# Dummy products at the start, an earlier end of attention, and block sums held back, in a hybrid flow step on one core

## The chip, the cores and the metric

The kernel runs on one core of a Trainium2 chip. The metric is the device time of one launch in microseconds (us). A core has five engines that this text names by the profile's words: PE (matrix products), DVE and ACT (vector and scalar work), POOL (a slower vector engine, which here also issues some DMAs) and SP (which issues most DMAs).

## The reference, cut to what matters

The program is one inference step of two layers over 640 tokens (512 latent tokens in a grid of 8 x 64, and 128 prompt tokens) of width 1024. All data are float32. Layer 0 mixes tokens by attention, layer 1 by a gated linear recurrence; a gated feed-forward stage (width 2816) follows each.

```python
def layer(ctx, lat, i):
    # six modulation vectors per group: silu(cond) @ w_mod[i] + b_mod[i]
    xm_c, xm_l = modulate(rms_norm(ctx)), modulate(rms_norm(lat))   # shift and scale
    if i == 0:
        # prompt: softmax(q k^T / 8) v over the 128 prompt tokens, 16 heads of 64
        # latent: softmax over a window of 8 rows x 16 columns (+ bias table)
        #         and over 256 cached keys of the context
        o_c, o_l = attention(xm_c, xm_l, cache_k, cache_v) # then @ attn_w_o
    else:
        o_c, o_l = recurrent_block(xm_c, xm_l, state_h)    # then @ lru_w_out
    ctx, lat = ctx + g1 * o_c, lat + g1 * o_l
    for x in (ctx, lat):                                   # feed-forward
        gate, up = split(modulate(rms_norm(x)) @ w_gu[i])
        x += g2 * ((silu(gate) * up) @ w_down[i])
```

The outputs are both groups of tokens after a last norm, the new keys and values of the prompt, and the last states of the recurrence.

## The kernel before

Activations lie transposed: eight tiles of 128 features by 640 tokens (`x`), and a product is made in two chunks of 320 tokens. A float32 product is made as three products of a shorter type: each operand is split into a high part (a cast, on ACT) and a low part (operand less high part, on DVE), and PE adds high x high, high x low and low x high (`some`, L221 to L223; `split`, L1305). One such instruction of 320 columns follows the last after 0.147 us.

**The start** (`pe` at L318, `act` at L324, `dve` at L321 record each instruction in the order in which it is written). While `x` arrives, PE adds up squares for the norm. The first four vectors of modulation come from `vectors` (16 products of 256 columns for each of two halves `h` and two kinds `j`, one of each as soon as its weights `sw` have landed), are copied by ACT to `row` and brought into columns by `coefficients` (products `at<-sel,row`). The squares are summed over features by five products of `ssq` with a column of ones (`at<-ones,ssq`), DVE and POOL make the reciprocal root `rs` and the diagonal tiles `dg`, and `spread` brings them to all partitions (`kk<-dg,ones`). `normed` on DVE and `high` on ACT then make the first operand of the first real products. `keep(2)` issues two products of the conditioning vector with the identity, into columns of `aux` that nobody reads.

**Attention** goes over eight pairs of heads `p`. For each, `qk` makes queries and keys of the pair, and splits them: casts `KS<-K` on ACT (L796), low parts into `KZ` on DVE (L797), and a DMA that brings each half to the other partitions (L799; on POOL's queue for pairs 0 and 7). `attend` goes over four blocks of 128 latent tokens, two at a time: for each block scores (L821, L822), score read on DVE (L827), exponential on ACT (L830), scaling, four transposes (L839) and their copy `PT` on ACT (L841). `softmax_prompt` does the like for the prompt's 128 tokens (L856 to L869), and `heads_out` multiplies with the values (`op`, L917) and copies to `O`. The first output products with `wo` stand behind the last pairs: `O` of the first seven pairs is split into `ohi` and `olo` after pair 6, pinned behind `self.parted`, the last key cast and the last low part of pair 7, so that the splits of the output do not come ahead of what pair 7 waits for. `project` then multiplies with `wo`; three output tiles are accumulated at once while pair 7 is still in its softmax.

**The feed-forward stage of layer 1** is made by halves with block sums: `x` is cut into four blocks (features 0 to 511 and 512 to 1023, tokens 0 to 319 and 320 to 639: B11, B12, B21, B22). `second_half(k)` splits B12 and B22 of tile `k` (`halve`), and `sums(k)` makes differences of the blocks on DVE (L999 to L1001) and POOL (L1002, `t4`), which are split too. `sum_weights` makes sums of the weights' blocks on POOL (L1057), behind `t4` of the second tile (`self.pw`). The products are at L1136 to L1138.

What stands in which order on an engine is set by the order of the source, by a scheduler that moves ready work of one engine ahead by its own estimate of time, and by pins (`pin`, `issue_after`): an instruction so marked comes behind the one named. Each engine then works its queue in that order, and an instruction that waits holds all behind it.

Of the kernel before, what the change touches and what calls it, by code (L numbers as in the profile page):

```python
# [125 lines left out]
class _Step:  # L126
# [169 lines left out]
    def start(self, hi, lo, sp, big):  # L296
# [97 lines left out]
        dve(nc.vector.tensor_scalar, v, aux[:, 256:256 + NT], 1.0 / D, EPS, ALU.mult, ALU.add)  # L394
# [5 lines left out]
        vectors(0, pm, 1, 1)  # L400
        row = rows(0, pm)
# [40 lines left out]
        keep(2)  # L442
# [147 lines left out]

    def project(self, w, hi, lo, gk, nxt=None, done=None, ahead=False):
        G = self.need(self.gcols, gk)
        for f in range(KT):
            u = self.unit(w[f], "m" if ahead else None)
            for t0, t1 in CH:
                self.residual(f, t0, t1, self.chunk(u, hi, lo, t0, t1, not ahead or f > 1), G, nxt)
                if nxt:
                    self.scale(f, t0, t1, *nxt)
            if done:
                done(f)  # L600
        if nxt:
            self.stats()
            self.shift(*nxt)
# [161 lines left out]
    def keys_tile(self):  # L765
        nc = self.nc
        K = self.t([P, 960], F32, "K", 1)

        def ek(t0, s, ps):
            if t0 == 0:  # L770
                nc.scalar.copy(K[:, 0:320], ps)
                nc.vector.tensor_copy(K[:, 512:576], ps[:, 0:64])
            else:
                nc.scalar.copy(K[:, 320:512], ps[:, 0:192])
                nc.vector.tensor_copy(K[:, 832:960], ps[:, 192:320])
        return K, ek

    def qk(self, p, hi, lo, ap, Q=None, K=None):
# [11 lines left out]
        KZ = self.kz[p % 2]  # L790
        pairs = [(QS, Q, [Q, Q]), (KS, K, [KZ[:, 0], KZ[:, 1]])]
# [8 lines left out]
        self.parted = low, cast  # L800
# [46 lines left out]
    def softmax_prompt(self, QS, KS, KZ, ap):  # L847
# [20 lines left out]
        pt = self.t([P, 256], F32, "PT", 5, ap)  # L868
# [3 lines left out]
    def attend(self, p, QS, KS, KZ, V, O, ap):  # L872
# [4 lines left out]
        for a in range(2):  # L877
# [104 lines left out]
    def halve(self, n, k, v):  # L982
        self.split(self.X[n + "h"][:, k], self.X[n + "l"][:, k], v)
# [5 lines left out]
    def second_half(self, k, key):  # L989
        b12, b22 = [self.x[:, j, HT:NTOK] for j in (k, k + KH)]  # L990
        for j, n, v in ((k, "B12", b12), (k + KH, "B22", b22)):
            self.normed(j, HT, NTOK, key)
            self.halve(n, k, v)

    def sums(self, k, xd):
# [3 lines left out]
        nc.vector.tensor_tensor(b11, b12, b11, ALU.subtract)  # L999
# [305 lines left out]
    def split(self, hi, lo, v, after=(None, None)):  # L1305
        with self.pin(after[1]):
            self.nc.scalar.copy(hi, v)  # L1307
        with self.pin(after[0]):
            self.nc.vector.tensor_tensor(lo, v, hi.bitcast(F32), ALU.subtract)  # L1309
# [22 lines left out]
    def run(self):  # L1332
# [35 lines left out]
        with self.phase("attn", tp=2, sp=2, op=1, quota=24) as ap:  # L1368
# [7 lines left out]
            with self.pin(self.parted[0]):  # L1376
                padded(1)
            self.vq(0, xhi, xlo, V)
            for p in range(8):
# [101 lines left out]
```

## Time and profile before

| | us |
|---|---|
| runs | 1521.42, 1522.43, 1522.82 (median 1522.43) |
| profiled execution, its own time | 1522.34 |
| its span | 1520.6 |
| PE busy | 1491.0 (98%) |
| DVE, ACT, POOL busy | 1062.4 (70%), 697.9 (46%), 253.2 (17%) |

The profile shows one execution. Its page gives each engine's busy time and the costliest groups of instructions. From the trace come three more views: a timeline (start in us, length, engine, line, operation, output<-input, count, and in brackets the idle time before and what ended it), busy time by stretch (start:end, length, busy time and count of PE's instructions, granted clock of PE as a share of full speed, share of DMA engines at work, GB/s), and groups. Where rows of one kind follow each other they are one row with a count; two matrix instructions stand for one float32 product, and three lines for one split product.

### The profile page before, as it was taken

The numbers are of one execution on the slowest core, as the hardware profiler recorded it, in microseconds if no ns is written. First come the engines' busy times: TensorE is split into PE (matmuls) and PEld (weight loads), VectorE is DVE, ScalarE is ACT, GpSimd is POOL, SyncE is SP. The second block draws the span as 40 slices with busy tenths as digits, with TensorE's granted clock in tenths as the row PEclk, the third lists the DMA queues.
The fourth block names the chain that finished last, engine by engine and source line by source line (L and its number), as shares of the span: only waits on it lengthen the run. The fifth ranks groups of instructions, "written<-read, shape, count | busy, mean of one in ns | idle before, by whom it ended". The sixth has DMA issues, their size and how long they took to land. (4 is left out here: it accounts for less than half of the span.)

```text
span 1520.6 us, 26091 instructions
## 1 busy us (share of the span) xinstructions
PE 1491.0 (98%) x10359; PEld 1443.9 (95%) x10359; DVE 1062.4 (70%) x2005; ACT 697.9 (46%) x1268; POOL 253.2 (17%) x276
## 2 busy tenths in 40 slices
PE   8999999899999999999999999999999999999997
PEld 6999999899999999999999888899999999999997
DVE  5778998769999987434443769985965656566555
ACT  4576666754332123312321478864634342434243
POOL 0112132100111110000000114220322323222211
PEclk9999999999999999999999999999999999999999
DMA  9545665336566664222222443335342231323211
GB/s 379 165 142 162 188 188 172 117 136 187 179 190 197 207 195 134 62 84 84 65 64 92 145 131 109 119 104 175 97 125 83 71 111 56 100 67 98 70 56 70
DMA packets 72330, 196.65 MB, mean 129 GB/s; under 512 B 8048, under 2 KB 24592, under 8 KB 72080
## 3 DMA queue, kind: packets, MB, share of 16 engines
q1 hardware_dynamic: 57392, 142.32, 29.7%
q0 software_dynamic: 14240, 51.98, 11.2%
q8 instruction: 81, 1.33, 0.4%
q10 hardware_dynamic: 576, 0.68, 0.1%
q14 instruction: 41, 0.34, 0.1%
HBM read 179.48 MB, written 8.92 MB: 124 GB/s over the span
## 5 line engine op out<-in xcount | busy, mean ns | idle before, releaser
L221 PE MATMUL mm<-big,whi 128*128 128x320 f32 (+3 forms) x1233 | 383.7, 313 | 6.5 <-ACT big L1307 5.3
L222 PE MATMUL mm<-big,whi 128*128 128x320 f32 (+3 forms) x1233 | 383.7, 312 | 0.4 <-DVE big L564 0.2
L223 PE MATMUL mm<-big,wlo 128*128 128x320 f32 (+3 forms) x1233 | 383.9, 312 | 0.0
L221 PEld LDWEIGHTS mm<-big,whi 128*128 128x128 f32 x1233 | 232.8, 189 | 9.2 <-ACT big L1307 6.0
L222 PEld LDWEIGHTS mm<-big,whi 128*128 128x128 f32 x1233 | 233.3, 189 | 2.8 <-DVE big L1309 0.7
L223 PEld LDWEIGHTS mm<-big,wlo 128*128 128x128 f32 x1233 | 232.9, 189 | 1.5
L250 DVE SCALAR_TENSOR_TENSOR mprod<-mraw,csb 128x1024 f32<-128x1024 f32 x160 | 195.1, 1219 | 12.3 <-DMA mraw<-in_wm 11.8
L587 DVE SCALAR_TENSOR_TENSOR x<-mm,G,x 128x320 f32<-128x320 f32 (+2 forms) x192 | 77.9, 436 | 83.7 <-PE mm L223 83.5
L180 ACT CAST whi<-raw 128x1024 fp32r<-128x1024 f32 (+1 forms) x71 | 73.9, 1041 | 108.6 <-PE mm L222 62.4
L182 DVE TENSOR_TENSOR wlo<-raw,whi 128x1024 fp32r<-128x1024 f32 (+1 forms) x87 | 106.0, 1219 | 21.6 <-ACT whi L180 12.5
L221 PE MATMUL mm<-big,whx 128*128 128x320 f32 (+3 forms) x348 | 108.3, 311 | 0.0
L223 PE MATMUL mm<-big,wlx 128*128 128x320 f32 (+3 forms) x348 | 108.0, 310 | 0.0
L222 PE MATMUL mm<-big,whx 128*128 128x320 f32 (+3 forms) x348 | 107.8, 310 | 0.0
L246 POOL DMA_DIRECT2D mraw<-in_wm x80 | 43.1, 538 | 364.8 <-DVE mprod L250 270.5
L221 PE MATMUL mx<-big,whi 128*128 128x320 f32 (+3 forms) x287 | 89.4, 311 | 0.0
L223 PE MATMUL mx<-big,wlo 128*128 128x320 f32 (+3 forms) x287 | 89.1, 311 | 0.0
L222 PE MATMUL mx<-big,whi 128*128 128x320 f32 (+3 forms) x287 | 88.9, 310 | 0.0
L221 PE MATMUL mx<-big,whx 128*128 128x320 f32 (+3 forms) x260 | 80.6, 310 | 0.0
L223 PE MATMUL mx<-big,wlx 128*128 128x320 f32 (+3 forms) x260 | 80.5, 310 | 0.0
L180 ACT CAST whx<-raw 128x1024 fp32r<-128x1024 f32 (+1 forms) x40 | 41.1, 1029 | 85.5 <-PE mm L222 47.9
L222 PE MATMUL mx<-big,whx 128*128 128x320 f32 (+3 forms) x260 | 80.3, 309 | 0.0
L1307 ACT CAST whi<-raw 128x1024 fp32r<-128x1024 f32 (+1 forms) x41 | 41.3, 1008 | 73.2 <-PE mm L222 44.9
(347 smaller groups left out, 3721.5 us busy)
## 6 DMA issues: line engine op xcount, KB each, us to landing
raw<-in_gu SPq DMA_DIRECT2D x88, 512.0 KB, 3.5
mraw<-in_wm POOLq DMA_DIRECT2D x80, 512.0 KB, 3.9
raw<-in_dn SPq DMA_DIRECT2D x24, 512.0 KB, 3.6
sw<-in_wm SPq DMA_DIRECT2D x16, 512.0 KB, 10.7
raw<-in_wqk SPq DMA_DIRECT2D x16, 512.0 KB, 5.0
raw<-in_wi SPq DMA_DIRECT2D x16, 512.0 KB, 3.6
whi<-in_wi POOLq DMA_DIRECT2D x16, 512.0 KB, 4.1
raw<-in_dn SPq DMA_DIRECT2D x16, 448.0 KB, 3.3
```

The lines of the kernel that those rows point to most:

```text
L180: nc.scalar.copy(hi, raw)
L182: nc.vector.tensor_tensor(lo, raw, hi.bitcast(F32), ALU.subtract)
L221: nc.tensor.matmul(ps, hi[:, k], xhi[:, k, s], start=(k == 0), stop=False)
L222: nc.tensor.matmul(ps, hi[:, k], xlo[:, k, s], start=False, stop=False)
L223: self.done = nc.tensor.matmul(ps, lo[:, k], xhi[:, k, s], start=False, stop=(k == last)).ins
L246: nc.gpsimd.dma_start(w, self.i["wm"][l * 6 + j - 2, f])
L250: nc.vector.scalar_tensor_tensor(prod, w, 1.0, self.csb[:, s], ALU.mult, ALU.mult, accum_out=out[:, s, f:f + 1])
L587: self.nc.vector.scalar_tensor_tensor(xs, ps[:, a - t0:b - t0], G[:, s, f:f + 1], xs, ALU.mult, ALU.add)
L1307: self.nc.scalar.copy(hi, v)
```

## The change

It has three parts.

1. At the start, two dummy products are added ahead of each half of the first vectors, two ahead of the coefficients, and one more behind `spread`. The five column sums are made with 32 columns of ones instead of one, and the variance is read from the first column of each.
2. At attention's end, the softmax of the prompt of pairs 6 and 7 goes with the first two blocks instead of the last two, and has a buffer of its own (`PP`). The first unit of `wo` is requested ahead of the keys' products of pair 7 (`opening`). The cast of the first output tile is pinned behind the copy of the second half of the keys (`self.copied`) instead of the last key cast, and its low part is free; those of the other heads stay where they were.
3. In layer 1's feed-forward stage, the first subtraction of each `sums(k)` is pinned behind the last low part of the second half (`self.halved`).

```diff
-    def ws(self, w, xhi, xlo, evac, fill=1, ch=CH):
+    def ws(self, w, xhi, xlo, evac, fill=1, ch=CH, also=None):
         u = self.unit(w)
+        if also:
+            also()
...
+        keep(2)
         vectors(0, pm, 0, 0)
+        keep(2)
         vectors(0, pm, 0, 1)
         for j, b in enumerate(blocks):
-            pe(aux[:, 256 + j:257 + j], self.ssq[:, b:b + P], self.ones[:, 0:1], start=True, stop=True)
+            pe(aux[:, 288 + 32 * j:320 + 32 * j], self.ssq[:, b:b + P], self.ones[:, 0:32], start=True, stop=True)
...
         vectors(0, pm, 1, 0)
         vectors(0, pm, 1, 1)
+        keep(2)
         row = rows(0, pm)
...
         spread()
-        keep(2)
+        keep(3)
...
+    def opening(self):
+        self.first = self.unit(self.i["wo"][0], "m")
+
     def project(self, w, hi, lo, gk, nxt=None, done=None, ahead=False):
         G = self.need(self.gcols, gk)
         for f in range(KT):
-            u = self.unit(w[f], "m" if ahead else None)
+            u = self.first if ahead and not f else self.unit(w[f], "m" if ahead else None)
...
-                nc.scalar.copy(K[:, 320:512], ps[:, 0:192])
+                self.copied = nc.scalar.copy(K[:, 320:512], ps[:, 0:192]).ins
...
-            self.ws(self.i["wqk"][KT + p], hi, lo, ek, 0)
+            self.ws(self.i["wqk"][KT + p], hi, lo, ek, 0, CH, self.opening if p == 7 else None)
...
-        self.parted = low, cast
+                self.parted.append((low, cast))
...
-        pt = self.t([P, 256], F32, "PT", 5, ap)
+        pt = self.t([P, 256], F32, "PP", 1, ap)
...
+        ppt = None
         for b0 in (0, 2):
             pts = [self.softmax(p, b, QS, KS, KZ, bts, ap) for b in (b0, b0 + 1)]
-            ppt = self.softmax_prompt(QS, KS, KZ, ap) if b0 else None
+            if (b0 == 0) == (p > 5):
+                ppt = self.softmax_prompt(QS, KS, KZ, ap)
             self.heads_out(p, b0, pts, ppt, V, cv, self.ps("op"), O)
...
-            self.halve(n, k, v)
+            self.halved = self.halve(n, k, v)
...
-        nc.vector.tensor_tensor(b11, b12, b11, ALU.subtract)
+        with self.pin(self.halved):
+            nc.vector.tensor_tensor(b11, b12, b11, ALU.subtract)
...
-                        self.split(ohi[:, k], olo[:, k], O[:, k], self.parted)
+                        self.split(ohi[:, k], olo[:, k], O[:, k], self.parted[-1] if k else (None, self.copied))
```

Lines move with the change: L318 becomes L320, L796 becomes L805, L821 becomes L830, L867 becomes L876, L917 becomes L928, L999 to L1002 become L1011 to L1014, L1057 becomes L1069, L1098 becomes L1110, L1136 to L1138 become L1148 to L1150, and L1307 and L1309 become L1319 and L1321.

How the order on the engines changes is shown at three places. On PE at the start, before (`ss<-sw,csp` are the halves of `vectors`, `mm<-big,whi` is the first real product):

```order
L318 MATMUL ss_190<-sw_19_114,csp_101 32x256 x4
L318 MATMUL ss_190<-sw_20_116,csp_101 32x256 x4
L318 MATMUL at_159<-ones_72,ssq_166 128x1 x5
L318 MATMUL ss_190<-sw_21_118,csp_101 32x256 x4
L318 MATMUL ss_190<-sw_22_120,csp_101 32x256 x4
L318 MATMUL at_159<-sel_104,row_218 128x2 x4
L318 MATMUL kk_220<-dg_208,ones_72 128x128 x4
L318 MATMUL kk_221<-dg_208,ones_72 128x128
L318 MATMUL at_159<-csp_101,ident_63 128x256 x2
L318 MATMUL mm_265<-big_85,whi_123 128x320
```

and now:

```order
L320 MATMUL at_159<-csp_101,ident_63 128x256 x2
L320 MATMUL ss_190<-sw_19_114,csp_101 32x256 x4
L320 MATMUL at_159<-csp_101,ident_63 128x256 x2
L320 MATMUL ss_190<-sw_20_116,csp_101 32x256 x4
L320 MATMUL at_159<-ones_72,ssq_166 128x32 x5
L320 MATMUL ss_190<-sw_21_118,csp_101 32x256 x4
L320 MATMUL ss_190<-sw_22_120,csp_101 32x256 x4
L320 MATMUL at_159<-csp_101,ident_63 128x256 x2
L320 MATMUL at_159<-sel_104,row_224 128x2 x4
L320 MATMUL kk_226<-dg_212,ones_72 128x128 x4
L320 MATMUL kk_227<-dg_212,ones_72 128x128
L320 MATMUL at_159<-csp_101,ident_63 128x256 x3
```

The dummy products (`at<-csp,ident`) stand ahead of both halves, ahead of the coefficients and, one more, ahead of the first real product. Nothing else has moved.

On ACT at the end of attention, from the copy of the second half of pair 7's keys (L774), before:

```order
L774 COPY K_3770<-mm_3804 128x192
L180 CAST whi_4250<-raw_4248 128x1024
L841 COPY PT_3660<-tp_3655 128x512
L796 CAST KS_3834<-K_3770 64x960 x2
L1307 CAST big_3847<-big_561 128x640
L869 COPY PT_3682<-tp_3677 128x256
L1307 CAST big_3847<-big_561 128x640 x6
```

and now, from the same copy (L782) on:

```order
L782 COPY K_3777<-mm_3817 128x192
L1319 CAST big_3860<-big_568 128x640
L843 ACTIVATE S_3640<-S_3640,rc_3645 128x512
L850 COPY PT_3638<-tp_3633 128x512
L805 CAST KS_3847<-K_3777 64x960 x2
L1319 CAST big_3860<-big_568 128x640 x5
```

The first output cast stands ahead of the key casts; the softmax of pair 6's last blocks (L843, L850) follows it, and goes on behind these rows. On PE, pair 7's first scores (L830, L831) stand now behind the first products of three output tiles and ahead of the rest:

```order
L223 MATMUL mm_4122<-big_3860,whi_3786 128x320
L223 MATMUL mm_4152<-big_3860,whi_3786 128x320
L223 MATMUL mm_4190<-big_3860,whi_4186 128x320
L830 MATMUL sp_3892<-KS_3847,QS_3846 128x512
L831 MATMUL sp_3892<-KZ_80_576,QS_3846 128x512
L830 MATMUL sp_3893<-KS_3847,QS_3846 128x512
L831 MATMUL sp_3893<-KZ_80_576,QS_3846 128x512
L224 MATMUL mm_4122<-big_3861,whi_3786 128x320
```

On DVE at the block sums, before (`xt` and `big_10850` are the low parts of the halves, L999 to L1001 the sums):

```order
L999 TENSOR_TENSOR x_10854<-x_10854 128x320 x2
L1309 TENSOR_TENSOR xt_10865<-x_10854,xt_10865 128x320
L1309 TENSOR_TENSOR big_11467<-g_11529,big_11466 128x320
L1000 TENSOR_TENSOR c_1861_11772<-x_10854 128x320
L1001 TENSOR_TENSOR x_10854<-x_10854 128x320
L1309 TENSOR_TENSOR xt_10865<-x_10854,xt_10865 128x320
L1000 TENSOR_TENSOR c_1865_11839<-x_10854 128x320
```

and now:

```order
L1321 TENSOR_TENSOR big_10857<-x_10861,big_10857 128x320 x3
L1321 TENSOR_TENSOR xt_10872<-x_10861,xt_10872 128x320
L1321 TENSOR_TENSOR big_10857<-x_10861,big_10857 128x320
L1011 TENSOR_TENSOR x_10861<-x_10861 128x320 x4
L1321 TENSOR_TENSOR big_11474<-g_11591,big_11473 128x320
L1012 TENSOR_TENSOR c_1861_11779<-x_10861 128x320
L1013 TENSOR_TENSOR x_10861<-x_10861 128x320
```

All low parts of the halves (four of `xt`, the last of `big_10857` for B22) stand ahead of the first subtraction, where subtractions and low parts alternated before.

More of the change, by code (lines that the diff above doesn't have):

```diff
@@ L388, in start @@
         pm = self.ps("ss")
+        keep(2)
         vectors(0, pm, 0, 0)
+        keep(2)
         vectors(0, pm, 0, 1)
         for j, b in enumerate(blocks):
-            pe(aux[:, 256 + j:257 + j], self.ssq[:, b:b + P], self.ones[:, 0:1], start=True, stop=True)
+            pe(aux[:, 288 + 32 * j:320 + 32 * j], self.ssq[:, b:b + P], self.ones[:, 0:32], start=True, stop=True)
         v = self.t([P, 8], F32, "var", 2)[:, 0:NT]
-        dve(nc.vector.tensor_scalar, v, aux[:, 256:256 + NT], 1.0 / D, EPS, ALU.mult, ALU.add)
+        dve(nc.vector.tensor_scalar, v, aux[:, 288:288 + 32 * NT].rearrange("p (j c) -> p j c", c=32)[:, :, 0], 1.0 / D, EPS, ALU.mult, ALU.add)
         rs = self.t([P, 8], F32, "rs", 2)[:, 0:NT]
@@ L790, in qk @@
         KZ = self.kz[p % 2]
+        self.parted = []
         pairs = [(QS, Q, [Q, Q]), (KS, K, [KZ[:, 0], KZ[:, 1]])]
@@ L982, in halve @@
     def halve(self, n, k, v):
-        self.split(self.X[n + "h"][:, k], self.X[n + "l"][:, k], v)
+        return self.split(self.X[n + "h"][:, k], self.X[n + "l"][:, k], v)
     def first_half(self, k, key):
@@ L1308, in split @@
         with self.pin(after[0]):
-            self.nc.vector.tensor_tensor(lo, v, hi.bitcast(F32), ALU.subtract)
+            return self.nc.vector.tensor_tensor(lo, v, hi.bitcast(F32), ALU.subtract).ins
     def lru_gate(self, f, hi, lo, lp, after=None):
@@ L1375, in run @@
             QK = self.qk(0, xhi, xlo, ap, Q, K)
-            with self.pin(self.parted[0]):
+            with self.pin(self.parted[-1][0]):
                 padded(1)
```

## The prediction

> **What bounds the kernel now.** I read the page first, then busy time by stretch, then PE's timeline at every stretch where PE was not full.
>
> ```profile
> span 1520.6 us, 26091 instructions
> PE 1491.0 (98%) x10359; PEld 1443.9 (95%) x10359; DVE 1062.4 (70%) x2005; ACT 697.9 (46%) x1268; POOL 253.2 (17%) x276
> ```
>
> PE is busy for 98% of the span, so only three things can be won: PE's 29.6 us of idle time (1520.6 less 1491.0), time in which PE ran slowly, and PE work itself. The change removes no PE work and adds a little. The second of the three is seen in stretches of 3.41 us, cut where PE's granted clock turns. Columns: stretch, length, PE busy (instructions), granted clock, DMA share, GB/s.
>
> ```profile
> 14.27:17.68 3.41, 2.65 (x34) 0.99 1.02 414
> 17.68:21.10 3.42, 3.34 (x15) 0.50 1.03 420
> ...
> 290.75:294.16 3.41, 1.48 (x11) 0.99 0.06 19
> 294.16:297.57 3.41, 1.17 (x5) 0.50 0.59 170
> 297.57:300.99 3.42, 3.42 (x34) 0.51 0.44 128
> ...
> 847.12:850.53 3.41, 1.68 (x13) 1.00 0.73 210
> 850.53:853.95 3.42, 2.66 (x14) 1.00 0.59 178
> ...
> 1092.88:1096.29 3.41, 1.65 (x11) 0.99 0.33 108
> 1096.29:1099.71 3.42, 3.42 (x15) 0.51 0.33 95
> ```
>
> A stretch in which PE was busy for 1.65 us or less is followed by one at half clock; after 1.68 us or more the clock stays. The stretch from 14.27 seems to break this (2.65 busy, then half clock), but 1.28 of it are ten one-column products (below), a kind of work that seems not to count: 1.37 without them. So each half-clock stretch that is full of work costs 1.7 us, half of 3.42, and a wait of about 1.75 us within one stretch is enough to bring it on. The three parts of the change lie at three of these places.
>
> **Start: dummy products.** PE's rows before (columns here and below: start, length, engine, line, operation, output<-input, shape, count, and in brackets idle time before and what ended it):
>
> ```profile
> 12.69 0.64 PE L318 MATMUL ss<-sw,csp 128*32 128x256 f32 x8 [0.67 <-DMA sw<-in_wm]
> 13.87 0.64 PE L318 MATMUL ss<-sw,csp 128*32 128x256 f32 x8 [0.54 <-DMA sw<-in_wm]
> 14.44 1.28 PE L318 MATMUL at<-ones,ssq 128*128 128x1 f32 x10
> 15.64 1.40 PE L318 MATMUL ss<-sw,csp 128*32 128x256 f32 x16
> 17.76 1.86 PE L318 MATMUL at<-sel,row 128*128 128x2 f32 x8 [0.72 <-ACT row L324]
> 19.48 2.48 PE L318 MATMUL kk<-dg,ones 128*128 128x128 f32 x10
> 21.76 1.91 PE L318 MATMUL at<-csp,ident 128*128 128x256 f32 x4
> 23.16 0.78 PE L318 MATMUL mm<-big,whi 128*128 128x320 f32 x1
> ...
> 32.89 1.05 PE L318 MATMUL at<-sel,row 128*128 128x2 f32 x8
> ...
> 34.48 0.69 PE L318 MATMUL at<-csp,ident 128*128 128x256 f32 x2
> ...
> 21.57 1.68 DVE L321 TENSOR_TENSOR big<-big,kk 128x512 f32<-128x512 f32 x4 [1.48 <-PE kk L318]
> ```
>
> A dummy product is two instructions; at full clock a pair spans 0.69, and back to back I take 0.43 for each pair (at half clock two pairs end 1.91 after they start, less the tail of some 0.2, over four). The change puts two pairs (0.86) into the wait of 0.67 (+0.2), two into that of 0.54 (+0.3, with the first), two into that of 0.72 (nothing: the row copy on ACT is late by the same 0.5), and one pair more behind the row sums. Widening the column sums from 1 to 32 columns costs nothing that these rows could show (a two-column product at full clock takes 0.13). So the last modulation vector ends at 17.5 instead of 17.04, and the coefficients start at 18.3 instead of 17.76. If the clock holds, they take 1.05 instead of 1.86 and the row sums half of 2.48: they end near 20.4 instead of 21.76. DVE, which waits for them, starts near 20.3 instead of 21.57, and the first real product comes behind three pairs (1.3) near 21.9 instead of 23.16. **Start: -1.25.** Busy time that counts is then at least 2 us in any 3.41 us here, well above 1.68. It cannot be more than -2.0 (0.8 from the coefficients, 1.2 from the row sums, nothing paid for the dummies); if the clock drops all the same, the delay of 0.5 and one pair at half clock (0.7) are lost: +1.2.
>
> [...]
>
> **End of attention.** Rows before, around pair 7's last key casts and around the stage's end, and the groups of the last pair's softmax (columns of these: count, busy us, mean ns, idle before):
>
> ```profile
> 292.74 0.43 PE L867 MATMUL tp<-ident,S 128*128 128x128 f32 x2 [0.94 <-DVE S L866]
> 296.40 1.17 PE L221 MATMUL mm<-big,whi 128*128 128x320 f32 x3 [3.23 <-ACT big L1307]
> ...
> 321.72 0.43 PE L867 MATMUL tp<-ident,S 128*128 128x128 f32 x2 [1.47 <-DVE S L866]
> 322.62 0.88 PE L917 MATMUL op<-PT,big 128*64 128x128 f32 x12 [0.46 <-ACT PT L869]
> ...
> 324.73 0.42 PE L221 MATMUL mx<-big,whi 128*128 128x320 f32 x1
> ...
> 291.96 0.32 ACT L774 COPY K<-mm 128x192 f32<-128x192 f32 x1
> ...
> 293.59 2.01 ACT L796 CAST KS<-K 64x960 fp32r<-64x960 f32 x2
> ...
> 295.55 1.05 POOL L799 DMA_DIRECT2D KS<-KS  x2 [4.35 <-ACT KS L796]
> ...
> DMA to landing us min/median/max: 3.1/4.3/6.9
> ...
> L827 DVE CUSTOM_DVE_ANT_1 S<-sp,bt 128x512 f32<-128x512 f32 x6 | 4.2, 692 | 3.1 <-PE sp L822 2.3 <-issue 0.4 <-PE tp L839 0.3
> L830 ACT ACTIVATE S<-S,nm 128x512 f32<-128x512 f32 x8 | 5.8, 727 | 4.0 <-DVE nm L827 3.6 <-DVE rc L832 0.3
> L841 ACT COPY PT<-tp 128x512 f32<-128x512 f32 x8 | 4.5, 589 | 3.2 <-PE tp L839 3.2
> ```
>
> Four waits, 0.94, 3.23, 1.47 and 0.46, are 6.1 us. From 296.40 to 300.99 PE worked 4.6 us at half clock: another 2.3. Lost in all: 8.4. The wait of 3.23 is one for the first output cast, which stood behind both key casts (2.01) on ACT. In the change it stands ahead of them. Pair 6's prompt softmax is earlier too, and with it pair 7's key product, by some 4 us (the copy of its second half stood at 291.96 on ACT). Working on by these durations in the new order: the first output cast runs near 288.9 to 289.6, the key casts near 290.6 to 292.6, and PE has first output products and the rest of pair 6 until about 293.8, with 1.15 us of waits on the way.
>
> Then comes what the change adds. Pair 7's first scores stand in PE's queue ahead of the output products of heads 1 to 5, and need the swapped halves of the keys by DMA: issued by POOL behind the casts, near 293.1, landing 4.3 us later by the median, so near 297. PE idles for some 2.95 us with finished casts queued behind the scores. At the end nothing is left to cover the last two blocks: with the prompt's part gone forward, one block's chain (score read 0.69, exponential 0.73, copy 0.59, and some 1.5 for sum, reciprocal, scaling and four transposes between them: 3.5) stands behind another's 0.69 with two blocks' transposes as its only cover, and the block before it is covered in part. I count 4.75 in four waits from 310 to 321. Sum of the waits: 1.15 + 2.95 + 4.75 = 8.85 against 8.4. A half-clock stretch after the 2.95 is likely, but the products it slows are followed by waits for pair 7's softmax, which hide it; the transposes of the two prompt heads, moved into covered time, may give the 0.45 back. **End of attention: 0.** Lower bound -4.5: keys landing 1.2 earlier (3.1), the end's waits half of what I count (-2.4), and two of the small waits hidden (-0.9). Upper bound +3: two half-clock stretches (3.4) that nothing hides, less 0.45. The first request of wo comes earlier on SP's queue, ahead of pair 7's bias tables; those still land by 299, before scores are read.
>
> **Block sums.**
>
> ```profile
> 1095.77 0.41 PE L1137 MATMUL mm<-xt,whx 128*128 128x320 f32 x1 [1.76 <-DVE xt L1309]
> ...
> 1087.73 5.70 DVE L1309 TENSOR_TENSOR big<-x,big 128x320 fp32r<-128x320 f32 x4
> ...
> 1095.24 0.48 DVE L1309 TENSOR_TENSOR xt<-x,xt 128x320 fp32r<-128x320 f32 x1
> ...
> 1085.33 3.23 POOL L1002 TENSOR_TENSOR x<-x,c 128x320 f32<-128x320 f32 x2 [11.29 <-ACT x L980]
> 1088.51 1.55 POOL L1057 TENSOR_TENSOR sum<-raw 128x512 f32<-128x512 f32 x1
> ```
>
> PE waits 1.76 us for the last low part of a half (xt, done at 1095.7) and then works for 3.42 us at half clock: 1.7 more, 3.4 together. That low part is late because four operations of DVE took 5.70, 1.43 each, where one takes 0.48 (1095.24), all while POOL made the weight sums (1088.51 on, 1.55 each, four of them, until 1094.6). With the first subtraction pinned behind the last low part, all lows are done near 1087.5 (by the new order DVE has eleven operations up to the last of them from about 1083 on, 0.40 apart), five microseconds before PE wants the last of them (1095.77 less the wait and the clock: 1092.4). Wait and half clock go: -3.4. What is late next: POOL's work starts only behind the subtractions, near 1089.4, and its weight sums run from 1092.6 to 1098.6. If they slow DVE by the same factor, four or five operations of 0.40 become 1.43 ahead of the product g<-mm that frees a PSUM buffer: g then comes near 1098.4, and the next chunk, which before began at 1101.5, wants that buffer near 1097.6: a wait of about 0.8. **Block sums: -2.6**, bounds -3.9 (no slowing, and a phase of the clock that spares the next gap) and +1 (six or more slow operations, a wait of 2.7 and a half-clock stretch after it).
>
> **Sum**: -1.25 + 0 - 2.6 = -3.85 against the profiled execution's own 1522.34 (1520.6 of span and 1.7 around it), which is 0.09 under the median of the runs shown: **1518.5**. Beyond it, the two feed-forward stages see small reorderings, and the grid of 3.41 us stands elsewhere against the gaps that stay near the line (847.12: 1.68), 1.7 for each that changes sides. [...]
>
> **Rivals.** *All three gains in full.* Keys land in 3.1, the clock holds everywhere: -1.25 - 3.1 - 3.4 gives 1514.6. For it: the minimum is in the rows, and each gap then is under 1.75. Against: an ordering that leaves PE's next ready work behind a DMA. *The contention only moves.* POOL's sums hit DVE as before, g comes three microseconds late and block sums give 0: 1521.1. For it: 5.70 for four operations; against: fewer urgent operations are left then. *Scores block PE* (the other side). Pair 7's scores wait for keys that land in 6.9: +2.6, the wait of 5.6 brings two half-clock stretches (3.4), and the end's waits, then unbroken, a third (1.7): +7.7, in all 1526.2, slower. It decides from a landing of about 6 us on. Against: the POOL queue carries little at that time. *Dummies that do not hold the clock*: start +1.2 instead of -1.25, 1520.9.
>
> **How the numbers follow.** Forecast 0.42 (its own range 1516.5 to 1520.5), all gains 0.22, contention moved 0.16, scores blocking 0.10, dummies useless 0.10. The range 1513.8 to 1522.6 leaves out the blocking and the far ends of the others. A change of 0.2% is 3.0 us, what a measurement here can tell: faster means below 1519.4. That takes seven tenths of the forecast (0.30), nearly all of the second case (0.21) and 0.05 of the third and fifth: 0.56. Slower (above 1525.5): 0.09. The rest, 0.35, is no change.
>
> **What would show it.** Start: the coefficient products near 1.05 and the first real product near 21.9, no clock of 0.5 before 25 us. Attention: PE's wait of 3.23 for the output cast gone and one for KS in front of L830 (old L821), the first mx product of the output projection within 1 us of 324.73 less the start's gain. Block sums: no wait before L1149 (old L1137) for xt and full clock there, POOL's L1069 near 1092.6, and a wait of under 1 us for a PSUM buffer near 1097. I am wrong if the start's clock still falls, if KS lands much sooner or later than 4.3 us after its issue, or if DVE's operations stay at 0.4 beside POOL's sums.

## The result

The changed kernel is slower: median 1526.78 us (16 runs, 1523.03 to 1530.07) against 1522.48 us before (16 runs, 1520.9 to 1526.9), a ratio of 1.0023 with a 95% interval of 1.0014 to 1.0032, or +3.5 us (2.1 to 4.9). The forecast was 1518.5 us, so both the sign and the range were wrong. The profiled execution of the changed kernel took 1524.77 us (span 1523.0), 2.0 us less than the median of its runs.

To see where the time went, the start of the same PE instruction is compared in both traces: the n-th split product (high x low behind high x high) of the program, so that moves within a stage do not matter. A minus is a lead of the changed kernel.

| in the kernel before, at | changed less before, us | what lies ahead of it |
|---|---|---|
| 74.93 | -1.07 | the start |
| 232.08 | -1.04 | attention to pair 5 |
| 347.74 | +4.63 | attention's end and the first products behind it |
| 842 | +4.61 | first feed-forward stage |
| 1003.47 | +5.90 | recurrent layer |
| 1081.53 | +4.39 | its output projection |
| 1102.68 | +0.82 | block sums, first chunks |
| 1120.27 | +2.47 | block sums, the chunks behind |
| 1496.18 | +2.41 | the rest |

The start won 1.05 and the block sums 1.9 net (3.6, and 1.65 given back). Attention's end lost 5.7. The 1.3 lost in the recurrent layer and the 1.5 won in its output projection lie where the change edits nothing; the 1.5 is a stretch from 1021.2 us that the trace before has at half clock (0.50) and the trace after at full (1.00).

### The profile page after: what moved, and what is told of

The parts are those of the page before. It is cut to its first block, busy times and chain, and to the rows that moved or that the text cites. A ratio compares the mean times of both kernels' runs of the same rounds, so it can differ in the third digit from the quotient of the medians.

```text
span 1523.0 us, 26118 instructions
## 1 busy us (share of the span) xinstructions
PE 1493.0 (98%) x10373; PEld 1441.4 (95%) x10373; DVE 1064.1 (70%) x2005; ACT 698.4 (46%) x1268; POOL 256.4 (17%) x276
## 5 line engine op out<-in xcount | busy, mean ns | idle before, releaser
L1319 ACT CAST whi<-raw 128x1024 fp32r<-128x1024 f32 (+1 forms) x41 | 41.3, 1008 | 69.7 <-PE mm L224 44.2
```

## The profile after

The page: PE's busy time grew by 2.0 us, of which the dummies are a part.

```profile
span 1523.0 us, 26118 instructions
PE 1493.0 (98%) x10373; PEld 1441.4 (95%) x10373; DVE 1064.1 (70%) x2005; ACT 698.4 (46%) x1268; POOL 256.4 (17%) x276
```

The start, PE's timeline. The coefficients take 0.95 instead of 1.86, the row sums 1.36 instead of 2.48, and the first real product comes at 21.77 instead of 23.16.

```profile
17.22 1.13 PE L320 MATMUL at<-csp,ident 128*128 128x256 f32 x4
18.19 0.95 PE L320 MATMUL at<-sel,row 128*128 128x2 f32 x8
19.00 1.36 PE L320 MATMUL kk<-dg,ones 128*128 128x128 f32 x10
20.20 1.46 PE L320 MATMUL at<-csp,ident 128*128 128x256 f32 x6
21.77 0.42 PE L320 MATMUL mm<-big,whi 128*128 128x320 f32 x1
```

Attention's end: all PE rows from 286 to 330 us with a wait that the trace names, and the rows of ACT and POOL that answer to those before.

```profile
292.23 0.71 PE L223 MATMUL mm<-big,whi 128*128 128x320 f32 x3 [0.24 <-ACT big L1319]
295.42 0.68 PE L830 MATMUL sp<-KS,QS 128*128 128x512 f32 x1 [2.48 <-DMA KS<-KS]
297.14 0.77 PE L830 MATMUL sp<-KS,QS 128*128 128x512 f32 x1 [0.61 <-PE sp L831]
307.97 0.66 PE L848 MATMUL tp<-ident,S 128*128 128x128 f32 x4 [0.24 <-ACT PT L850]
312.77 0.66 PE L848 MATMUL tp<-ident,S 128*128 128x128 f32 x4 [0.29 <-ACT PT L850]
322.43 0.63 PE L848 MATMUL tp<-ident,S 128*128 128x128 f32 x4 [0.80 <-DVE S L845]
324.11 0.63 PE L848 MATMUL tp<-ident,S 128*128 128x128 f32 x4 [1.04 <-DVE S L845]
325.41 0.66 PE L928 MATMUL op<-PT,big 128*64 128x128 f32 x8 [0.68 <-ACT PT L850]
...
287.70 0.73 ACT L1319 CAST big<-big 128x640 fp32r<-128x640 f32 x1
289.42 2.01 ACT L805 CAST KS<-K 64x960 fp32r<-64x960 f32 x2
...
291.38 0.53 POOL L808 DMA_DIRECT2D KS<-KS  x1 [7.54 <-DVE nm L836]
...
292.15 0.52 POOL L808 DMA_DIRECT2D KS<-KS  x1
```

POOL requests the two halves of the swapped keys at 291.38 and 292.15. By the trace they land at 295.28 and 297.05, 3.9 and 4.9 us later. The first scores start 0.14 us after the first landing. The second ones start 0.09 us after the second landing, so I take the wait of 0.61 as one for KS too, though the row names PE's own product.

The same place in stretches of 3.41 us, cut where the granted clock turns (columns as before: length, PE busy, clock, DMA):

```profile
291.96:295.37 3.41, 0.74 (x4) 1.00 1.02 245
295.37:298.78 3.41, 2.75 (x7) 0.52 0.70 162
298.78:302.20 3.42, 3.42 (x15) 0.50 0.00 0
319.26:322.68 3.42, 2.62 (x20) 1.00 0.33 40
322.68:326.09 3.41, 1.69 (x20) 1.00 1.03 411
326.09:329.50 3.41, 3.41 (x28) 0.52 0.81 322
```

The named waits come to 6.4 us, hardly more than the 6.1 before. But three stretches at half clock stand where two stood (294.16 to 300.99): two follow the waits for KS (295.37 to 302.20, clock 0.52 and 0.50), and a third the waits in pair 7's last blocks (326.09 to 329.50, clock 0.52). Counted against the start-to-start times of the same products at full clock (0.147 us for 320 columns, 0.235 for 512, 0.055 for 128, 0.11 for a transpose), about 16 us are lost between 283.6 and 329.6, against about 11 between 287 and 325 before. Around the keys (to 302) it is a little over 7 us in both. The difference lies behind: some 2.7 us more of short gaps between 306 and 321, where before products of `wo` stood between, 3.1 in the three last waits against 2.5, and 1.8 of half clock behind them.

The block sums: PE has no wait for the low part any more. DVE's slow operations beside POOL's sums now stand at 1100 us (1.39 us each for three of them, against 0.48 to 0.49), and the next wait is 1.36 us for a product g. This stage starts 4.4 us later than before (the row of 1081.53 above), so 4.4 has to be taken off these times to set them beside those of the kernel before.

```profile
1098.85 0.49 DVE L1110 TENSOR_TENSOR g<-mm,g 128x320 f32<-128x320 f32 x1
1099.25 0.78 DVE L1321 TENSOR_TENSOR big<-c,big 128x320 fp32r<-128x320 f32 x1
1099.95 4.16 DVE L1321 TENSOR_TENSOR big<-x,big 128x320 fp32r<-128x320 f32 x3
1104.04 3.08 DVE L1012 TENSOR_TENSOR c<-x 128x320 f32<-128x320 f32 x2
...
1110.35 0.48 DVE L1110 TENSOR_TENSOR g<-mm,g 128x320 f32<-128x320 f32 x1
...
1094.73 6.04 POOL L1014 TENSOR_TENSOR x<-x,c 128x320 f32<-128x320 f32 x2 [16.31 <-DVE c L1012]
1100.73 1.52 POOL L1069 TENSOR_TENSOR sum<-raw 128x512 f32<-128x512 f32 x1
...
1110.89 0.42 PE L1148 MATMUL mm<-xt,whx 128*128 128x320 f32 x1 [1.36 <-DVE g L1110]
```

## Experiments

Single runs of one kernel spread over 4 to 10 us, so the table gives ratios to the kernel before, run on the same chip beside it, and the same in us of 1522.5. Each kernel has 12 runs unless it says otherwise. A ratio whose interval holds 1 is no difference that can be told.

| kernel | ratio [95%] | us |
|---|---|---|
| e1 start | 1.0020 [1.0004, 1.0035] | +3.0 |
| e2 attention's end | 1.0029 [1.0014, 1.0043] | +4.4 |
| e3 block sums | 0.9979 [0.9965, 0.9993] | -3.2 |
| e4 start, block sums | 1.0009 [0.9996, 1.0023] | +1.4 |
| e5 start, mprod pinned | 1.0002 [0.9990, 1.0013] | +0.3 |
| e6 start, block sums, mprod pinned | 0.9991 [0.9981, 1.0001] | -1.4 |
| e7 attention's end without the prompt | 0.9998 [0.9984, 1.0011] | -0.3 |
| e8 prompt of pairs 6 and 7 only | 1.0018 [1.0008, 1.0028] | +2.7 |
| e9 prompt of pair 6 only | 1.0008 [0.9996, 1.0020] | +1.2 |
| e10 whole change, pair 7's prompt left, mprod pinned | 0.9998 [0.9984, 1.0012] | -0.3 |
| e11 mprod pinned only | 0.9999 [0.9986, 1.0011] | -0.2 |
| e12 dummies without wide sums (one run) | 1526.3 us | - |
| e13 whole change without the prompt, mprod pinned | 0.9985 [0.9970, 1.0001] | -2.3 |

### The three parts apart

The first two theories: the parts add up as the lead in the traces says (A), or the earlier start shifts the later stages against the clock's stretches (B). Each kernel holds the lines of the diff for its part and no others.

```diff
 e1: + keep(2) / keep(2) / keep(2) / keep(3), column sums 32 wide
 e2: + prompt's softmax ahead for p > 5, opening(), first output cast behind self.copied
 e3: + first subtraction of sums(k) behind self.halved
 e4: e1 and e3 together
```

> Start alone: dummy products and wide column sums, nothing else. Theory A (the parts add up, as the lead of the changed kernel over the kernel before shows at each stage: -1.05 us after the start, +5.7 at attention's end, -3.6 and then +1.65 at the block sums): about 1.0 us faster, ratio 0.9993, no half clock before 25 us, the coefficient products at 0.95 us for eight. Rival B (the loss at attention's end comes from the stages being shifted by the earlier start against the clock's stretches of 3.41 us): start alone already loses some of it and comes out at 0 to +3 us, with waits at attention's end like before but more half-clock stretches.

> Attention's end alone. Theory A: slower by about 5.7 us (ratio 1.0037), with a wait of some 2.5 us of pair 7's first scores for KS, two half-clock stretches after it, and waits of 2.5 us in the last blocks with one half-clock stretch behind. Rival B: without the shift of the start it costs 0 to +2 us only.

> Block sums alone. Theory A: about 1.9 us faster (ratio 0.9987): the wait of 1.76 us for xt and the half-clock stretch go (-3.5), and one for the product g (about 1.4 us) comes some 15 us later. Rival B: a gap at another phase of the clock brings a half-clock stretch behind the new wait, and the gain is 0 to -0.5 us.

> Start and block sums without the change at attention's end. Theory A: -1.05 - 1.9 = about 3 us faster than before (ratio 0.998), and so about 5.7 us faster than the whole change. Rival B: as the whole change, since the shift of the start stays: within 2 us of it.

Attention's end and the block sums came out as theory A has them, within their intervals (+2.1 to +6.5, and -5.3 to -1.1). The start did not: alone it is 3.0 us slower. Its trace shows the start's lead (-1.27 at 75 us) kept until 309 us, and then +1.76 at 330 and +4.23 at 339. At that place, on DVE, POOL and PE of e1:

```profile
329.34 1.23 DVE L250 SCALAR_TENSOR_TENSOR mprod<-mraw,csb 128x1024 f32<-128x1024 f32 x1 [3.49 <-DMA mraw<-in_wm]
330.49 0.08 DVE L250 DVE_READ_ACCUMULATOR mprod<-mraw,csb 128x1 f32 x1
330.49 1.59 DVE L590 SCALAR_TENSOR_TENSOR x<-mm,G,x 128x320 f32<-128x320 f32 x4
...
324.03 1.08 POOL L246 DMA_DIRECT2D mraw<-in_wm  x2 [28.83 <-PE op L920]
...
331.09 0.63 PE L221 MATMUL mm<-big,whi 128*128 128x320 f32 x1 [2.58 <-DVE x L590]
...
331.02:334.43 3.41, 3.34 (x12) 0.50 0.00 0
```

`mprod` is a product on DVE for a modulation vector that is needed much later. It needs 512 KB that POOL's queue requests only when attention's last products are done. In the kernel before it stands behind the first residual updates (`x<-mm`, L587):

```profile
329.03 1.59 DVE L587 SCALAR_TENSOR_TENSOR x<-mm,G,x 128x320 f32<-128x320 f32 x4 [1.81 <-PE mm L223]
...
332.34 1.22 DVE L250 SCALAR_TENSOR_TENSOR mprod<-mraw,csb 128x1024 f32<-128x1024 f32 x1
```

With the start's edits, 300 us ahead of it, the scheduler put `mprod` first; that they changed its estimate of time is inferred from the order. DVE waits 3.49 us for the DMA, the four updates stand behind it, PE waits 2.58 us for the buffers that they free, and half clock follows, to about 337 us (0.50 from 331.02 to 334.43, 0.58 on the mean of 334.43 to 337.84).

### Start without its side effect

```diff
+            self.updated = self.nc.vector.scalar_tensor_tensor(xs, ...).ins   # in residual
...
+            if ahead and f == 1:                                               # in project
+                self.anchor = self.updated                                     # mod_cols issues behind it
```

> Start alone, and the modulation products of the first feed-forward stage (mprod) pinned behind the residual updates of the second output tile. Theory M (in the start-only kernel the scheduler put one mprod, which waits 3.5 us for its DMA, ahead of four residual updates on DVE; PE waited 2.6 us for them and fell to half clock; the start itself gives 1.3): the wait of the first full output product for x and the half clock behind it are gone, and the kernel is 1.0 to 1.4 us faster than before, 4 us faster than start alone. Rival C (the earlier start meets the clock's stretches or the DMAs of the first feed-forward stage badly, and mprod only shows it): still 1 us or more slower than before, with the wait taken over by another one near 328 us.

> Start and block sums, with the same pin. Theory M: the gains add: -1.2 - 2.7 = about 4 us faster than before (ratio 0.9974), and 5 us faster than start and sums without the pin. Rival C: no better than start and sums without the pin by more than 1 us.

> The pin of mprod alone, nothing of the change. With it the start's own worth can be read from the start with the pin (ratio 1.0002). Theory S (the start is worth its 1.1 us, and the pin costs as much): 1 us slower than before. Rival T (the pin costs nothing, and the start's lead is lost elsewhere): within 0.5 us of before.

The pin alone changes nothing that can be told (-0.2 us). With it, the start goes from +3.0 to +0.3, and start with block sums from +1.4 to -1.4: 2.7 us each time, though each difference is known to some 3 us only. PE's wait for the updates was 2.58 in e1's trace and 1.02 in e4's, where the DMA landed 3.8 us after its request instead of 5.3. In e5's trace the wait is gone and the lead is -1.97 at 330 us. Theory M holds for the loss; its 1.0 to 1.4 us of gain did not show. That the start is worth its 1.05 us in the whole kernel does not follow: 0.3 with an interval of -1.5 to +2.0 reaches to -1.1 only just.

### Attention's end in pieces

```diff
 e7: opening() and the first output cast as in the change; prompt's softmax as before
 e8: if (b0 == 0) == (p > 5)    # prompt's softmax ahead, in its own buffer PP, nothing else
 e9: if (b0 == 0) == (p == 6)   # the same for pair 6
```

> Attention's end without the prompt's softmax moved: first output cast ahead of the key casts and wo's first unit requested earlier, prompt softmax with the last two blocks as before. Theory P (the loss comes from the prompt's softmax being taken from the end, where it covered pair 7's last blocks: 2.65 us of short waits at 302 to 322, 0.7 more at 322 to 325 and 1.7 of half clock behind; the wait for KS costs no more than the wait for the output cast did): the loss is gone, -1 to +1 us against before. Rival K (the loss is the wait of pair 7's scores for KS at the head of PE's queue, 2.5 us, with two half-clock stretches behind): still 4 us or more slower.

> Only the prompt's softmax of pairs 6 and 7 moved ahead, casts and wo as before. Theory P: 3 to 5 us slower than before, with waits of three of the last blocks' transposes and copies at the end of about 2.5 us and a half-clock stretch at 326 to 330. Rival K: within 1.5 us of before.

> The prompt's softmax moved ahead for pair 6 only; pair 7 keeps it with the last two blocks. Theory P (the prompt's softmax of pair 7 was what covered its last blocks' chains): the end of the stage looks as before (waits of 1.5 and 0.5 us, full clock), and the kernel is between 1 us faster and 1 us slower than before. Rival Q (moving any prompt softmax ahead costs, because it delays that pair's last blocks on ACT and DVE): 1.5 to 3 us slower, with longer waits around 290 to 300 us.

The cast and the request of `wo` are neutral (e7: -0.3), the prompt's softmax costs (e8: +2.7). That fits theory P and not K. Rival Q can't be excluded by e9 (+1.2, -0.6 to +3.0): in its trace as in e8's, PE waits 3.1 to 3.2 us at the first scores of pair 7, since pair 7's keys come sooner and its scores stand early in PE's queue, where e7 has a wait of 2.06 for a cast and none for KS.

### Layer 0 alone

The spread of whole kernels comes in part from waits that no edit touches. Two rows show the kernel before and e5, in this order, at one and the same instruction of the recurrent layer, around which the order on every engine is the same in both:

```profile
978.92 1.32 PE L1265 MATMUL gp<-xc,gw 128*128 128x512 f32 x4 [1.07 <-issue]
```

```profile
980.40 1.99 PE L1270 MATMUL gp<-xc,gw 128*128 128x512 f32 x4 [2.15 <-ACT lt L1284]
```

Over the kernels run this wait was 1.07 to 2.28 us, and the four products behind it took 1.99 us in e5 against 1.32 before. So four kernels were cut off behind the first feed-forward stage.

```diff
-        xpool.close()
-        ... recurrent layer, second feed-forward stage, outputs
+        nc.vector.memset(self.st, 0.0)       # last state
+        ... self.x (after layer 0) to both token outputs
```

> The kernel before, cut off after the first feed-forward stage: the recurrent layer and everything behind it is left out (the last state is written as zeros, and the two token outputs hold the tokens after layer 0). It is the base for the three kernels that follow; about 850 us. If the spread of the runs (4 to 9 us in whole kernels) comes from the waits of the recurrent layer, the runs of this one agree within 2 us; if it comes from the start and attention, they spread as before.

> The same cut (recurrent layer and all behind it left out), with the start's dummies and wide sums and the pin of mprod. Theory S (the start keeps the lead of 1.05 us that the traces show at 75 us): 0.8 to 1.5 us faster than the cut kernel without it. Rival T (the lead is lost again before the first feed-forward stage ends): within 0.4 us of it, or slower.

> The same cut, with the whole change at attention's end. By the trace of the changed kernel (5.7 us lost there, of which about 2.3 are half-clock time that depends on where the clock's stretches fall): 3.5 to 5.7 us slower than the cut kernel without it.

> The same cut, with the prompt's softmax moved ahead for pair 7 only. Theory P (pair 7's prompt softmax covered its last blocks): 2 to 4 us slower than the cut kernel without it, most of what the whole change at attention's end costs. Rival Q (it is pair 6's that costs, or the two together): within 1 us of it.

| cut kernel | runs, us | median |
|---|---|---|
| t0 before | 862.97, 863.38, 864.74, 865.42, 866.94 | 864.74 |
| t1 start, mprod pinned | 863.20, 863.24, 863.28, 863.59 | 863.26 |
| t2 attention's end | 867.44 to 868.86 (4 runs) | 867.64 |
| t3 prompt of pair 7 only | 865.64 to 868.57 (4 runs) | 868.02 |

With the start and its pin the median falls by 1.5, the way theory S has it, but two of t0's five runs are as fast as t1's, so with four and five runs this gain is not clear of the noise. What is clear is that t1's runs agree within 0.4 us where those of t0 spread over 4. So the expectation that the spread comes from the recurrent layer alone was wrong: layer 0 has its own, and the start with the pin takes most of it away. In t0's profiled run, one of the two fast ones, the clock stayed full without dummies (1.00 from 10 to 30 us):

```profile
18.39 1.05 PE L318 MATMUL at<-sel,row 128*128 128x2 f32 x8 [0.72 <-ACT row L324]
```

where e2, also without dummies, had it at half (0.50 from 16.5 to 22.5 us):

```profile
18.39 1.87 PE L320 MATMUL at<-sel,row 128*128 128x2 f32 x8 [0.72 <-ACT row L326]
```

The whole change at attention's end costs 2.9 us here, a little less than expected, and all of t2's runs lie above all of t0's. Pair 7's prompt softmax alone costs as much (3.3). In t3's trace PE waits as the changed kernel does at the end, and is at half clock behind (0.56 on the mean of 325.22 to 328.00):

```profile
322.73 0.63 PE L839 MATMUL tp<-ident,S 128*128 128x128 f32 x4 [1.39 <-DVE S L836]
323.92 0.63 PE L839 MATMUL tp<-ident,S 128*128 128x128 f32 x4 [0.56 <-DVE S L836]
325.22 0.86 PE L919 MATMUL op<-PT,big 128*64 128x128 f32 x8 [0.68 <-ACT PT L841]
...
325.22:328.00 2.78, 2.78 (x29) 0.56 1.03 411
```

So moving pair 7's prompt alone is enough for the loss: theory P holds, and Q in the form put ahead of t3 does not. Two things limit this. In t3, too, the scheduler put `mprod` ahead of the updates (DVE waited 2.15 us for its DMA at 333.20), but PE waited only 0.27 us for them. And what pair 6's prompt costs stays open: e9 cannot tell, no cut kernel moves it alone, and e10 below speaks for some cost.

### The wide column sums, and what is left of the change

```diff
 e12: the four keeps, column sums 1 wide as before
```

> The dummy products at the start without the wide column sums. Theory W (one-column products hardly count as work for the clock, so both edits are needed): with the dummies alone, the stretch that holds the column sums has 1.3 us less that counts, but still more than 1.7 us: full clock all the same, and coefficients in 0.95 us. If the clock is at 0.5 before 25 us, the column sums count as idle and more of the stretch is idle than the rows say. The kernel as a whole is slower than before, like the start alone.

In its one profiled execution the clock is full throughout the start (1.00 from 10 to 30 us), and the coefficients take 0.95 us: the dummies alone are enough there. Theory W expected that too, so this run does not decide whether one-column products count for the clock. That they hardly count is an estimate from two traces in which the clock fell. In the kernel before, the stretch that holds them had 2.65 us busy (14.27 to 17.68), 1.52 without them, and was followed by 0.50; in e2 it had about 2.7 (12.7 to 16.1), 1.6 without them, and was followed by 0.50 too. Without them both lie under the 1.65 that was followed by half clock at 1092.88. In t0, which kept the clock, PE has waits of 0.26 and 0.72 us here, where the kernel before has 0.67, 0.54 and 0.72. Elsewhere in the traces before and after, no stretch at full clock with more than 1.69 us busy was followed by half clock. In e12 the stretch with the one-column products was busy throughout (3.41 from 14.27 to 17.68, some 2.2 of it other work). As a whole e12 is slow (1526.3 us): in its trace 2.9 us are lost at `mprod`, which stands in front like in the start alone, and 6.2 in the recurrent layer.

```diff
 e10: all three parts; prompt's softmax ahead for p == 6 only; mprod pinned
 e13: all three parts; prompt's softmax as before; mprod pinned
```

> The whole change with two mends: the prompt's softmax of pair 7 stays with its last blocks, and the modulation products of the first feed-forward stage are pinned behind the residual updates. By theories M and P: the two losses (2.7 to 3 us each) are gone, 3.5 - 5.5 = about 2 us faster than before and 5 us faster than the whole change. Rival: they are no more than what single profiles show, and it stays within 1.5 us of the whole change, 2 us or more slower than before.

> The whole change without the moved prompt softmax, and with mprod pinned behind the residual updates. If the parts add as measured one by one (start with the pin -1.4 in the cut kernels, attention without the prompt's softmax -0.3, block sums -3.2): about 4.5 us faster than before, ratio 0.997, the fastest of all. If they do not add (the start with the pin and the block sums together came out at -1.4 only): 1 to 2 us faster, no better than block sums alone.

e10 is 3.8 us better than the whole change, with pair 6's prompt and the wait for KS still in it. Its trace still loses 3.5 us at attention's end (-0.61 at 232 us, +2.88 at 348), with a half-clock stretch at 323.4 (eight `op` products take 1.07 us there, and 0.61 at 317.98), where e13's wins 2.0. The two kernels differ in pair 6's prompt (and its buffer) alone; over the runs they are 2.0 us apart, which is within the noise. e13 is 5.8 us better than the whole change and 2.3 us faster than before, the latter not clear of the noise; the parts do not visibly add up to the 4.5 that they came to one by one, but its interval (-4.6 to +0.2) holds that sum. Block sums alone (e3) beat both kernels by a margin that is clear of the noise: 3.2 us under the kernel before, 6.7 under the change. Nothing run was measurably better than that.

## Why the prediction was wrong, point by point

- **The start, -1.25.** Right in mechanism and size within the stage. The lead at 75 us was 1.07; over nine traces with dummies it is 0.63 to 1.68, mean 1.10, and over ten without them the same instruction stands between 0.70 ahead of the kernel before and 0.94 behind it, mean 0.27 behind: 1.4 between them. The reading by which the dummies act, that a stretch with little PE work is followed by half clock, held: the granted clock fell to 0.5 before 25 us in nine of the ten traces without dummies (0.50 in the kernel before, e2 and e7), and in none of the nine with them (1.00 in the changed kernel and in e12). What I had not seen is that it does not fall in every execution without them (t0: 1.00). How much of the lead a whole kernel keeps is not shown: e5 is at +0.3 us, -1.5 to +2.0.
- **"The two feed-forward stages see small reorderings."** This was a step without a price, and it failed. One row moved on DVE's order cost the start alone more than the start wins: +3.0 instead of -1.25, 2.7 of it back by a pin. The order on DVE showed `mprod` ahead of the updates before any run (that nothing else has moved holds for PE's rows at the start, not for DVE here), and I left out the DMA that it waits for. In the whole change it cost little: the DMA landed 3.8 us after its request there (5.3 in e1), DVE waited 1.98 us for it, and PE has a wait of 0.25 near it. So this step does not explain the whole kernel's loss.
- **End of attention, 0.** This is the step that decided. Its sum set 8.85 us of waits, and no half clock, against 6.1 of waits and 2.3 of half clock before. The named waits came to 6.4 instead, but with some 4.8 us of half clock (by the same count about 2.5 before) and some 2.7 us more of short gaps. What failed first is the sentence that the half clock behind the wait of 2.95 is hidden by waits for pair 7's softmax, which left nothing for it in the sum, nor for a stretch at the end. Nothing hid it: two stretches came behind the waits for KS (0.52 and 0.50, as two of 0.50 and 0.51 did before behind the wait for the cast), and a third behind the last waits (0.52). The second failure is the end: four waits of 4.75 from 310 to 321 were counted, and five named ones of 3.05 came, with the short gaps beside them, because the last blocks' chains no longer had the prompt's work as cover and most products of `wo` had been worked off before 307. The loss was 5.7 in the trace and 4.4 over the runs, against an upper bound of +3. The wait for KS itself was near its 2.95 (2.48 and 0.61), partly by luck: from the times put down for it (request near 293.1, 4.3 us to land, PE free at 293.8) it comes to 3.6, not 2.95, and PE was free 0.9 earlier, the request 0.9 to 1.7 earlier.
- **Block sums, -2.6.** Right in mechanism. Alone they are worth -3.2 (-5.3 to -1.1); in the changed kernel's trace it was -3.6 for the wait and the half clock, 1.65 given back, and so -1.9. With the 4.4 us by which the stage is later taken off, the low parts were done at 1087.3 (forecast 1087.5), but POOL's weight sums began at 1096.3 and not at 1092.6, since its two `t4` took 6.04 instead of 3.23 beside DVE. So DVE's slow operations (1.39 and 1.54 us each) missed the g that was forecast to be late (1094.5 instead of 1098.4) and came ahead of the next one: PE waited 1.36 us for it, where 0.8 was the forecast.
- **The rivals.** The one on the slower side named the right place and price order (scores block PE, half-clock stretches, the end's waits unbroken), but made it hang on a KS landing of 6 us or more. KS landed 3.9 and 4.9 us after its requests, near the 4.3 of the forecast, and it came out slower all the same: the condition was wrong, and its chance of 0.10 too small. The rival by which the contention only moves came in part (1.65 of 3.6). None of the three things named as making the forecast wrong came about; of the signs named for it, the first mx product showed the failure (328.28, where it was to be within 1 us of 324.73 less the start's gain).
- **Half clock behind a wait of about 1.75 us in one stretch.** Near enough for the sum of the waits: one of 2.48 with a second of 0.24 near it (0.74 us busy in the stretch from 291.96) was followed by half clock, and so were two of 1.04 and 0.68 in one stretch (322.68: 1.69 us busy, 1.72 idle).

## What to carry to other kernels

When an order is made by a scheduler, a local edit can move a waiting instruction hundreds of microseconds away: compare the orders of all engines, and for each moved row ask what it waits for and what stands behind it; a pin on that row is cheap. Work that may be done early is often what covers a dependent chain at a stage's end, so before it is pulled ahead, ask what fills the engine there, and price each wait with the half-clock time that may follow it (here two stretches at 0.52 and 0.50 behind the waits of 2.48 and 0.61). Where runs spread by more than the effect, measure a part alone in a kernel that is cut off behind it.

## What was not expected of the hardware

- Half clock can outlast one stretch: after 0.74 us of work in 3.41, the next stretch had 2.75 us busy at half clock, and the one behind it stayed at half clock too (0.50, 298.78 to 302.20). In the kernel before, one with 1.17 us busy at half clock was likewise followed by another (294.16 and 297.57). Behind the other half-clock stretches of both traces (3.36 to 3.42 us busy) the full clock came back, and in e10 behind one of 2.95 (323.37, by the length of its products), but for one at the start of the kernel before: 3.34 us busy, eight two-column products among them, and 0.51 in the next stretch (17.68 and 21.10).
- 1.69 us of work in a stretch was followed by half clock (322.68), where 1.68 had kept the full clock in the kernel before (847.12). So the line between 1.65 and 1.68 that the prediction took does not hold for both traces; why, no run shows.
- DVE's operations and POOL's were longer beside each other, and not always on the same side: DVE's took 1.39 us each (4.16 for three, against 0.48) and 1.54 (3.08 for two) beside POOL's weight sums of 1.52, and POOL's two `t4` took 6.04 (4.95 and 1.12) against 3.23 (2.13 and 1.13) in the kernel before, with DVE's own operations at 0.49. e3 has the same: 4.16 for three, 3.08 for two, and 6.03 for the two `t4`. Beside the sums a DVE operation takes about as long as one POOL operation (1.39 and 1.54 against 1.52; before, 1.43 against 1.55). Why that is so, and why a `t4` of 1.12 us took 4.95, many times one DVE operation of 0.49, no run here shows.
